# Attention's softmax work in larger pieces with two visits each, the last values projections moved to the end, and ScalarE's order fixed

## The chip, the cores and the metric

The program runs on one core of a Trainium2 chip. The metric is the device time of one execution in microseconds. Of three runs of the kernel before, the median is 2897.22 us (2896.98 to 2899.64). The core's engines are TensorE (PE in the profile, its weight loads PEld), VectorE (DVE), ScalarE (ACT), GpSimd (POOL) and SyncE (SP), which issues the DMAs here. Each engine works through its own list of instructions in the order in which they stand, and waits for others by semaphores.

## The reference

Two decoder layers over a sequence of 1024 tokens of width 1024, all in float32. Layer 0 mixes tokens by dilated sliding-window attention, layer 1 by a gated linear recurrence; behind each mixer stands a squared-ReLU MLP, and behind each of the four sub-layers `x <- LayerNorm(alpha * x + sublayer(x))`. The change lies in the attention:

```python
proj = (x @ w_in).reshape(B, S, 3, 3, 16, 64)        # 3 groups x (q, k, v) x 16 heads x 64
for g, (window, dilation) in enumerate(((128, 1), (512, 4), (2048, 16))):
    q, k, v = rotary(proj[:, :, g, 0]), rotary(proj[:, :, g, 1]), proj[:, :, g, 2]
    # sequence regrouped by residue mod dilation, in blocks of 128 queries;
    # a block sees itself and the block before it in its class
    s = where(in_band, q_block @ k_two_blocks.T / 8, -inf)
    m = max(s); p = exp(s - m); l = sum(p); o_g = (p / l) @ v_two_blocks; lse_g = m + log(l)
o = sum_g softmax_g(lse) * o_g                       # mixed per position and head
y = o @ w_out
```

## The kernel before

**Layout.** Heads are taken in 8 pairs of 128 rows (`NPAIR`). A *unit* is one pair in one of the three groups, so there are 24 units (`units`, L321), in the order group 2 (dilation 16), 1, 0 of pair 0, then of pair 1, and so on. Every unit has eight blocks of 128 queries. In group 2 a block sees only itself (128 keys); in group 1 every second block, and in group 0 all but the first, see 256 keys (`has_prev`, L464).

**Projections.** Two units make a group of work (L322). It needs six projections, taken as three pairs (keys and queries of the first unit, of the second, and the values of both), and each pair is computed with seven block products instead of eight (`ORDA`, L330). So `seq` (L331) has 12 groups x 7 x 3 = 252 products; the loop L732 takes one in a *slot*. A product is 12 matmuls of 128x512 (L646 to L648: each factor is split into a high and a low part of float32r, and three of the four partial products are kept). The x operands (`xh`, `xl`) of each of the seven are computed once, stored to DRAM (`xtd`) and loaded again for every later group (`get_T`, L375), 2 MB for each. Weights are loaded eight slots ahead, and split five slots ahead into a high part by ScalarE (L419) and three slots ahead into a low part by VectorE (L427).

**Inner work.** `pieces` (L461) cuts a unit into six pieces, which `at` hangs onto slots (`OFFS`, L55) of the next group: scores of two blocks (`qk`, L477, tile `s`), on VectorE mask, negative maximum and score in one instruction (L496), on ScalarE the exponential with its sum (L499), then the transposition of the probabilities on TensorE (`ptr`, L503, tile `ppt`) and its copy by ScalarE (L512), then the product with the values (`pv`, L515, tile `o`), copied to `og` by ScalarE (L532, L535). Values are transposed as well (`vtrans`, tile `vpt`). Maximum and sum are transposed (`combine_tr`, tile `mpt`), sent through DRAM to a layout with heads on rows, and `combine` (L566) makes of them the weights of the three groups, which six DMAs put into `frow`. `combine_mul` (L600) spreads them over the rows with a matmul (tile `fb`) and multiplies and adds on VectorE. PSUM has eight banks: three for the products (`mm`), two `s`, two `pt`, one `o`.

**The end.** The last group's two units can't begin before its projections are done. Their rotary steps, scores and all that follows (`tail`, L684, and the list `mine`, L782) are handed to `outproj_ln` (L849), which calls one entry at a time between the matmuls of the output projection (L179 to L181).

**What sets the order.** Inside the attention `in_order` (L103, L718) fixes TensorE and VectorE to the order in which the program writes the instructions; ScalarE, the DMAs and everything after the attention are placed by a scheduler.

## Time and profile before

| what | value |
|---|---|
| median of three runs | 2897.22 us |
| the profiled execution, its own time | 2893.09 us |
| span of its trace, first to last instruction | 2891.2 us |
| TensorE busy; its weight loads | 2785.1 us (96%); 2243.6 us (78%) |
| VectorE, ScalarE, GpSimd busy | 2084.2, 1450.7, 462.1 us |
| mean granted TensorE clock | 0.987 |
| attention's products (L646 to L648) | 7.98 to 1002.5 us |
| inner work, up to the last `fb` | 102.2 to 1097.5 us |

A timeline row has the start, the duration, the engine, the source line, the operation, what it writes and reads, and a count of instructions that were merged. In brackets stands the engine's idle time ahead of it and what ended that. Matmuls overlap, so the spacing of starts tells more than durations: a 128x512 matmul behind another starts 0.227 us after it at the full clock and 0.427 us after it at half. A float32 matmul of the inner work leaves two records in the trace; a transposition leaves one.

### The profile page before, as it was taken

The page shows a single profiled execution, that of the slowest core. Times are in us where ns is not written, and L with a number is a line of the kernel's source. Part 1 is how long each engine was busy: PE and PEld are TensorE (multiplying, and loading weights), DVE is VectorE, ACT ScalarE, POOL GpSimd, SP SyncE. Part 2 cuts the span into 40 slices and gives each one's busy share as a digit, 9 for nine tenths or more (in the row PEclk, how much of TensorE's full clock was granted, in tenths as well). Part 3 has the DMA queues.
Part 4 walks back from the last instruction along what each step waited for, and adds up shares of the span by engine and source line. Part 5 has one row for each costly group of instructions (what it writes and reads, how often), then busy time and mean ns, then how long its engine had stood idle before and what let it go on. Part 6 is the DMA issues. An engine that isn't in the chain of part 4 may idle for free. (4 is left out here: it accounts for less than half of the span.)

```text
span 2891.2 us, 40330 instructions
## 1 busy us (share of the span) xinstructions
PE 2785.1 (96%) x14152; PEld 2243.6 (78%) x14152; DVE 2084.2 (72%) x3685; ACT 1450.7 (50%) x3104; POOL 462.1 (16%) x211
## 2 busy tenths in 40 slices
PE   7899999999999998999999999999999999999998
PEld 6677777777777766788877887788888788877887
DVE  7677676777777667786688777456567787678777
ACT  5354555555455553645454434455553644454433
POOL 0111111111111102100053511111001200025310
PEclk9999999999999998999999999999999999999999
DMA  8876776678577533364484653111131455484654
GB/s 334 304 262 195 245 250 240 227 272 284 184 243 260 196 101 127 136 219 160 157 313 131 229 174 108 44 59 55 52 121 67 159 200 175 157 272 160 225 177 136
DMA packets 218043, 535.63 MB, mean 185 GB/s; under 512 B 30832, under 2 KB 45168, under 8 KB 217840
## 3 DMA queue, kind: packets, MB, share of 16 engines
q1 hardware_dynamic: 217840, 533.05, 54.1%
q8 instruction: 111, 1.82, 0.3%
q14 instruction: 92, 0.75, 0.1%
HBM read 408.96 MB, written 98.44 MB: 175 GB/s over the span
## 5 line engine op out<-in xcount | busy, mean ns | idle before, releaser
L646 PE MATMUL pmm<-xh,H 128*128 128x512 f32 x1008 | 410.2, 407 | 13.6 <-ACT H L419 8.0
L647 PE MATMUL pmm<-xl,H 128*128 128x512 f32 x1008 | 399.5, 396 | 12.3 <-DMA xl<-xtd 11.8
L648 PE MATMUL pmm<-xh,H 128*128 128x512 f32 x1008 | 398.6, 395 | 1.2 <-DVE H L427 1.2
L457 POOL TENSOR_TENSOR rot<-rot,sinT 128x1024 f32<-128x1024 f32 x48 | 137.7, 2873 | 861.0 <-DMA rot<-e 485.4
L646 PEld LDWEIGHTS pmm<-xh,H 128*128 128x128 f32 x1008 | 192.8, 191 | 54.6 <-ACT H L419 8.0
L647 PEld LDWEIGHTS pmm<-xl,H 128*128 128x128 f32 x1008 | 192.7, 191 | 52.6 <-DMA xl<-xtd 14.4
L648 PEld LDWEIGHTS pmm<-xh,H 128*128 128x128 f32 x1008 | 191.9, 190 | 43.8 <-DVE H L427 2.2
L496 DVE CUSTOM_DVE_ANT_0 p<-s,mask 128x128 f32<-128x128 f32 (+1 forms) x384 | 113.2, 348 | 142.3 <-PE s L485 132.5
L1226 PE MATMUL pdy<-dT,dS 128*128 128x512 f32 x512 | 201.4, 393 | 11.2 <-DVE dT L134 11.1
L499 ACT ACTIVATE p<-p,stats 128x128 f32<-128x128 f32 (+1 forms) x384 | 169.1, 443 | 65.9 <-DVE stats L496 65.5
L1227 PE MATMUL pdy<-dT,dS 128*128 128x512 f32 x512 | 200.6, 392 | 0.0
L1223 PE MATMUL pdy<-dT,dS 128*128 128x512 f32 x512 | 200.5, 392 | 0.0
L133 ACT ACTIVATE dS<-dr 128x512 fp32r<-128x512 f32 x192 | 120.1, 625 | 101.7 <-PE pdy L1227 45.3
L134 DVE TENSOR_TENSOR dS<-dr,dS 128x512 fp32r<-128x512 f32 x192 | 156.6, 815 | 10.7 <-ACT dS L133 10.7
L512 ACT ACTIVATE pts<-ppt 128x256 f32<-128x256 f32 (+1 forms) x192 | 85.9, 474 | 144.8 <-PE ppt L509 142.0
L167 PE MATMUL pmm<-f0nh,wh 128*128 128x512 f32 x384 | 152.7, 398 | 0.0
L169 PE MATMUL pmm<-f0nh,wl 128*128 128x512 f32 x384 | 150.4, 392 | 0.0
L168 PE MATMUL pmm<-f0nl,wh 128*128 128x512 f32 x384 | 149.8, 390 | 0.0
L1208 POOL TENSOR_TENSOR hold<-hold 128x512 f32<-128x512 f32 x32 | 52.2, 1632 | 568.3 <-DVE dT L134 290.8
L134 DVE TENSOR_TENSOR dT<-hold,dT 128x512 fp32r<-128x512 f32 x128 | 123.8, 967 | 3.7 <-ACT dT L133 3.7
L1226 PEld LDWEIGHTS pdy<-dT,dS 128*128 128x128 f32 x512 | 97.1, 190 | 32.9 <-DVE dT L134 12.9
L133 ACT ACTIVATE dT<-hold 128x512 fp32r<-128x512 f32 x128 | 80.2, 626 | 82.5 <-POOL hold L1202 33.5
(395 smaller groups left out, 7178.6 us busy)
## 6 DMA issues: line engine op xcount, KB each, us to landing
xh<-xtd SPq DMA_DIRECT2D x154, 512.0 KB
xl<-xtd SPq DMA_DIRECT2D x154, 512.0 KB
dr<-hd SPq DMA_DIRECT2D x192, 256.0 KB
dr<-in_w_down_dram SPq DMA_DIRECT2D x128, 256.0 KB
rot<-e SPq DMA_DIRECT2D x192, 128.0 KB
wa<-in_w_up_dram SPq DMA_DIRECT2D x48, 512.0 KB
wa<-in_w_attn_dram SPq DMA_DIRECT2D x36, 512.0 KB
wb<-in_w_attn_dram SPq DMA_DIRECT2D x36, 512.0 KB
```

Of the source, the lines that this page charges most:

```text
L133: act(hi, raw, AF.Copy)
L134: nc.vector.tensor_sub(lo, raw, hi.bitcast(F32))
L167: nc.tensor.matmul(o, wh[:, k], xs.h(k), start=k == 0, stop=False)
L168: nc.tensor.matmul(o, wh[:, k], xs.l(k), start=False, stop=False)
L169: nc.tensor.matmul(o, wl[:, k], xs.h(k), start=False, stop=k == NK - 1)
L499: act(p[:, h, :n], p[:, h, :n], AF.Exp, bias=sS[:, 0, h, b:b + 1], scale=-1.0, accum_out=sS[:, 1, h, b:b + 1])
L646: nc.tensor.matmul(o, wh, hi[k // 2][:, c], start=begin and k == 0, stop=False, skip_group_check=True)
L647: nc.tensor.matmul(o, wh, lo[k // 2][:, c], start=False, stop=False, skip_group_check=True)
L648: nc.tensor.matmul(o, wl, hi[k // 2][:, c], start=False, stop=end and k == 3, skip_group_check=True)
L1223: nc.tensor.matmul(o[q], h, T_[:, L], start=begin, stop=False, skip_group_check=True)
L1226: nc.tensor.matmul(o[q], h, T_[:, R], start=False, stop=False, skip_group_check=True)
L1227: nc.tensor.matmul(o[q], l, T_[:, L], start=False, stop=end, skip_group_check=True)
```

## The change

1. `Inner` takes the place of `pieces`. A unit of group 2 is one piece of eight blocks, the others are two pieces of four. Each piece has two visits: `visit_a` (the product with the values of the piece before, then all scores of this piece, in two `s` and two `pt` banks; VectorE and ScalarE take its first half in this slot and its second half in the next), and `visit_b`, two to four slots later (all transpositions of the piece, with two blocks of 128 keys in one bank; ahead of the first piece's products the values' transpositions; behind the last piece the transposition of maximum and sum). 
2. The groups of products: the first ten hold three pairs as before, the next two only the keys and queries of two units each, and a thirteenth the values of the last four units. 252 products are left, but the x operands are loaded for 13 groups. The last four units keep their transposed probabilities in `ptk` tiles and run only the values' part behind the attention.
3. ScalarE's order is fixed as well, with the exception of the high parts of the weights (`loose`), which are emitted one slot later than before.
4. `combine` has five steps instead of three, and its last tile comes from the large pool; `fb` uses the `s` banks and `mpt` the `o` bank. The `p` and `pts` pools have four buffers instead of three, the large pool 49 instead of 50.

```diff
-NSLOT = 50
+NSLOT = 49
-MIX = (5, 6, 7, 10, 11, 12, 13, 14, 15)
+MIX0, NMIX = 3, 5
-OFFS = ((0, 2, 4, 7, 9, 11), (10, 12, 15, 17, 19, 21))
+LATER = {9: 1, 10: 1, 11: 3}
-    wp = ctx.enter_context(tc.tile_pool(name="wp", bufs=3))
+    wp = ctx.enter_context(tc.tile_pool(name="wp", bufs=4))
...
-        groups = [units[i:i + 2] for i in range(0, len(units), 2)]
+        groups = [[("qk", u), ("qk", u + 1), ("v", u)] for u in range(0, len(units) - 4, 2)]
+        groups += [[("qk", u), ("qk", u + 1)] for u in (len(units) - 4, len(units) - 2)]
+        groups.append([("v", len(units) - 4), ("v", len(units) - 2)])
...
+            def banks(self, c):
+                bl = self.chunks[c]
+                if self.g == 2:
+                    return [bl[k:k + 2] for k in range(0, 8, 2)]
+                if self.g == 1:
+                    return [(bl[0], bl[2]), (bl[1],), (bl[3],)]
+                return [(b,) for b in bl]
...
+            def qk(self, c):
+                qT, kT = res[self.u, 0], res[self.u, 1]
+                for half, bl in enumerate(self.halves(c)):
+                    sb = [bank("pt" if half else "s", "s") for _ in range(2)]
...
+            def pv(self, c):
...
+                for b in self.chunks[c]:
+                    if b % 4 == 0:
+                        o = bank("pt" if g == 2 and b else "o", "o")
...
-            act(fh, l, AF.Copy)
-            yield
+            f2 = U("f", F32R)
+            fh = f2[:16, :NG * P].rearrange("p (g t) -> p g t", t=P)
+            fl = f2[:16, 512:512 + NG * P].rearrange("p (g t) -> p g t", t=P)
+            yield
+            act(fh, l, AF.Copy)
+            yield
...
-                fb = bank("pt", "fb")
+                fb = bank("s", "fb")
...
+        def visit_a(u, c):
+            while pend:
+                pend.pop(0)()
+            inner[u].qk(c)
+            inner[u].soft(c, 0)
+
+        def visit_b(u, c):
+            w = inner[u]
+            w.ptr(c)
+            if not w.hold:
+                if c == 0:
+                    w.vtrans()
+                pend.append(lambda: w.pv(c))
+            if c == len(w.chunks) - 1:
+                w.stats()
...
+            base, length = begin_of[gi + 1], begin_of[gi + 2] - begin_of[gi + 1]
+            hold = us[0] >= len(units) - 4
+            todo = [(u, c) for u in us for c in range(1 if units[u][1] == 2 else 2)]
+            for k, (u, c) in enumerate(todo):
+                first = base + UNIT0 + LATER.get(gi, 0)
+                a = first + k * length // len(todo)
+                b = first + int((k + 0.57) * length / len(todo) + 0.5)
+                if c == 0:
+                    at(a, lambda u=u, hold=hold: begin_unit(u, hold))
+                at(a, lambda u=u, c=c: visit_a(u, c))
+                at(a + 1, lambda u=u, c=c: inner[u].soft(c, 1))
+                at(b, lambda u=u, c=c: visit_b(u, c))
...
-        order = in_order((mybir.EngineType.PE, mybir.EngineType.DVE))
+        order = in_order((mybir.EngineType.PE, mybir.EngineType.DVE, mybir.EngineType.Activation), loose)
```

**TensorE, the second unit (group 1 of the first pair).** Names: `s` scores, `ppt` transposed probabilities, `vpt` transposed values, `o` product with the values, `mpt` transposed maximum and sum; "..." stands for the products (`pmm`) between the visits. Before, its first ten inner rows:

```order
L485 MATMUL s<-kT,qT 128x128 x2
L485 MATMUL s<-kT,qT 128x256 x2
L473 MATMUL vpt<-ident,vT 128x128 x8
...
L524 MATMUL o<-pts,vn 64x128 x4
...
L485 MATMUL s<-kT,qT 128x128 x2
L485 MATMUL s<-kT,qT 128x256 x2
L509 MATMUL ppt<-ident,p 128x128 x6
...
L550 MATMUL mpt<-ident,stats 32x128
...
L524 MATMUL o<-pts,vn 64x128 x6
L485 MATMUL s<-kT,qT 128x128 x2
```

Now, the same unit's first piece and the beginning of its second:

```order
L572 MATMUL o<-pts,vn 64x128 x16
L507 MATMUL s<-kT,qT 128x128 x2
L507 MATMUL s<-kT,qT 128x256 x2
L507 MATMUL s<-kT,qT 128x128 x2
L507 MATMUL s<-kT,qT 128x256 x2
...
L538 MATMUL ppt<-ident,p 128x128 x12
L556 MATMUL vpt<-ident,vT 128x128 x8
...
L572 MATMUL o<-pts,vn 64x128 x12
```

The runs have become two to four times as long and stand in fewer places between the products; a visit begins either with `o` or `s`, or with transpositions alone.

**ScalarE, the first group of products.** `H` is the high part of the weights, `xh` that of x, `e` a product copied out of PSUM, `bsel` a constant copied once, `hc_e` one of the other layer's constants. Before:

```order
L419 ACTIVATE H<-wb 128x512
L440 ACTIVATE bsel<-selw 128x384
L673 ACTIVATE e<-pmm 128x512
L419 ACTIVATE H<-wb 128x512
L133 ACTIVATE xh<-xT_296 128x1024
L673 ACTIVATE e<-pmm 128x512
L133 ACTIVATE xh<-xT_297 128x1024
L1384 ACTIVATE hc_e<-hc_e 128x16
```

Now:

```order
L430 ACTIVATE H<-wb 128x512
L133 ACTIVATE xh<-xT_294 128x1024
L133 ACTIVATE xh<-xT_295 128x1024
L720 ACTIVATE e<-pmm 128x512
L430 ACTIVATE H<-wb 128x512
L720 ACTIVATE e<-pmm 128x512
L720 ACTIVATE vp<-pmm 128x512
L430 ACTIVATE H<-wb 128x512 x2
...
L452 ACTIVATE bsel<-selw 128x384
```

The copy of `bsel` has moved back behind the products of two more of the seven steps, and both `xh` stand ahead of the copies out of PSUM.

**TensorE, behind the attention's last product.** The products left out ("...") are those of the output projection. Before, around the last transposition of maximum and sum and the last weights' matmuls:

```order
L509 MATMUL ppt<-ident,p 128x128 x4
L524 MATMUL o<-pts,vn 64x128 x8
L550 MATMUL mpt<-ident,stats 32x128
L524 MATMUL o<-pts,vn 64x128 x8
...
L606 MATMUL fb<-frow,bsel 128x512 x3
...
L606 MATMUL fb<-frow,bsel 128x512 x2
```

Now, from the last transposition of maximum and sum:

```order
L591 MATMUL mpt<-ident,stats 32x128
L538 MATMUL ppt<-ident,p 128x128 x4
L572 MATMUL o<-ptk,vn 64x128
L538 MATMUL ppt<-ident,p 128x128 x4
L572 MATMUL o<-ptk,vn 64x128 x15
L650 MATMUL fb<-frow,bsel 128x512 x2
...
L572 MATMUL o<-ptk,vn 64x128 x12
...
L572 MATMUL o<-ptk,vn 64x128 x14
...
L572 MATMUL o<-ptk,vn 64x128 x16
...
L650 MATMUL fb<-frow,bsel 128x512 x2
```

Between `mpt` and the `fb` that need its result there stood 42 matmuls of the output projection and 8 of `o`; now 72 of the output projection stand there, 70 of `o`, 16 transpositions and five `fb` of the pair before.

## Rows read from the trace of the kernel before

**Rows 1.** The page's first part: busy time by engine.
```profile
PE 2785.1 (96%) x14152; PEld 2243.6 (78%) x14152; DVE 2084.2 (72%) x3685; ACT 1450.7 (50%) x3104; POOL 462.1 (16%) x211
```

**Rows 2.** TensorE's waits, 105 to 1002 us: total, times, longest.
```profile
PE o L524 <- ACT og L535: 9.8, 3, 3.8
PE pmm L647 <- DMA xl<-xtd: 4.9, 4, 2.0
PE ppt L509 <- ACT pts L512: 4.5, 6, 1.4
PE vpt L473 <- DVE og L607: 3.6, 3, 1.6
```

**Rows 3.** Timeline of TensorE: one visit with three kinds of work.
```profile
127.42 0.39 PE L648 MATMUL pmm<-xh,H 128*128 128x512 f32 x1
127.74 0.66 PE L524 MATMUL o<-pts,vn 128*64 128x128 f32 x8
128.33 0.71 PE L485 MATMUL s<-kT,qT 64*128 64x128 f32 x8
128.98 0.66 PE L509 MATMUL ppt<-ident,p 128*128 128x128 f32 x4
129.39 0.48 PE L646 MATMUL pmm<-xh,H 128*128 128x512 f32 x1
129.71 0.40 PE L647 MATMUL pmm<-xl,H 128*128 128x512 f32 x1
```

**Rows 4.** Timeline of TensorE: a longer run of `o`.
```profile
225.77 1.09 PE L524 MATMUL o<-pts,vn 128*64 128x128 f32 x16
226.79 0.50 PE L646 MATMUL pmm<-xh,H 128*128 128x512 f32 x1
```

**Rows 5.** Timeline of TensorE: one transposition alone between products.
```profile
151.32 0.39 PE L648 MATMUL pmm<-xh,H 128*128 128x512 f32 x1
151.55 0.27 PE L550 MATMUL mpt<-ident,stats 128*32 128x128 f32 x1
...
151.89 0.40 PE L647 MATMUL pmm<-xl,H 128*128 128x512 f32 x1
```

**Rows 6.** Timeline of ScalarE and TensorE, 254 to 258 us.
```profile
254.22 0.52 ACT L591 ACTIVATE fh<-ml 16x384 fp32r<-16x384 f32 x1 [4.29 <-DVE ml L587]
...
256.71 1.04 ACT L535 ACTIVATE og<-o 128x512 f32<-128x512 f32 x1
...
257.80 1.12 PE L524 MATMUL o<-pts,vn 128*64 128x128 f32 x8 [3.79 <-ACT og L535]
```

**Rows 7.** Timeline of ScalarE and TensorE, 39 to 46 us.
```profile
39.23 0.52 ACT L440 ACTIVATE bsel<-selw 128x384 fp32r<-128x384 f32 x1 [6.88 <-DMA selw<-in_bsel_dram]
...
41.75 0.80 PE L646 MATMUL pmm<-xh,H 128*128 128x512 f32 x1 [2.36 <-ACT xh L133]
43.01 0.79 PE L647 MATMUL pmm<-xl,H 128*128 128x512 f32 x1 [0.47 <-DVE xl L134]
...
45.05 0.79 PE L648 MATMUL pmm<-xh,H 128*128 128x512 f32 x1 [1.24 <-DVE H L427]
```

**Rows 8.** Busy time by stretch: PE, PEld, DVE, ACT, POOL, clock, DMA share, GB/s.
```profile
0.00:100.00 100.00, 77.49 (x300) 60.88 (x300) 75.56 (x107) 39.55 (x61) 10.02 (x13) 0.93 0.91 337
300.00:400.00 100.00, 100.00 (x597) 78.29 (x596) 69.58 (x149) 57.65 (x157) 10.96 (x4) 1.00 0.74 256
1080.00:1100.00 20.00, 12.72 (x30) 7.05 (x29) 14.75 (x30) 5.03 (x9) 0.00 (x0) 0.65 0.41 130
```

**Rows 9.** Timeline of TensorE: the last maximum and sum, and the first weights.
```profile
1072.74 0.28 PE L550 MATMUL mpt<-ident,stats 128*32 128x128 f32 x1
...
1092.38 1.19 PE L606 MATMUL fb<-frow,bsel 128*128 128x512 f32 x2 [2.12 <-DMA frow<-fl]
```

**Rows 10.** VectorE and ScalarE by line and shape, 105 to 1002 us.
```profile
L496 DVE CUSTOM_DVE_ANT_0 p<-s,mask 128x256 f32<-128x256 f32 x154 | 57.6, 423 | 36.3 <-PE s L485 36.1
L535 ACT ACTIVATE og<-o 128x512 f32<-128x512 f32 x28 | 30.3, 1081 | 40.9 <-PE o L524 40.9
```

More of the change, by code (lines that the diff above doesn't have):

```diff
@@ L114, in __exit__ @@
             for i in list(nc.cur_bb.bb.instructions)[self.first:]:
-                if i.engine in self.engines:
+                if i.engine in self.engines and i.name not in self.loose:
                     if i.engine in before:
@@ L469, in vtrans @@
                 for j in range(2):
-                    pt = bank("pt", "vpt")
+                    pt = bank("s", "vpt")
                     for i in range(4):
@@ L503, in ptr @@
-            def ptr(b):
-                p = st.pop(("p", b))
-                nb = 2 if has_prev(b) else 1
-                pt = bank("pt", "ppt")
-                for h in range(2):
-                    for i in range(nb):
-                        nc.tensor.transpose(pt[:, (h * nb + i) * P:(h * nb + i + 1) * P],
-                                            p[:, h, i * P:(i + 1) * P], ident)
-                pts = wp.tile([P, 512], F32, name="pts", tag="pts")
-                act(pts[:, :2 * nb * P], pt[:, :2 * nb * P], AF.Copy)
-                st["pt", b] = pts
@@ L547, in combine_tr, with stats @@
+            def stats(self):
+                combine_tr(self.pr, self.g, self.sS, ml[self.pr])
         def combine_tr(pr, g, sS, ml):
-            pt = bank("pt", "mpt")
+            pt = bank("o", "mpt")
             nc.tensor.transpose(pt[:32, 0:P], sS.rearrange("p w a b -> p (w a b)"), ident)
@@ L564, in combine_tr, with combine @@
                             md[w, h].rearrange("(r i n) -> i r n", r=d, i=8))
-        def combine(pr, ml):
+        def combine(pr, ml, frow):
             def cv(tl, g):
@@ L621, in attention, with at @@
         fill = {}
-        def at(slot, f):
-            fill.setdefault(slot, []).append(f)
+        def at(slot, f, first=False):
+            fill.setdefault(slot, []).insert(0 if first else len(fill.get(slot, [])), f)
         ep, acc, part = {}, {}, {}
@@ L691, in unit_work @@
                 ogs[pr] = [None] * NG
-            sS = small([P, 2, 2, 8], "stats", 3)
-            adds = {}
-            def rope_of(t):
-                res[a, t], adds[t] = rope(ep.pop((gi, a, 0 if t == 1 else 1)), g, "qT" if t == 0 else "kT")
-            def begin():
-                ogs[pr][g] = U("og")
-                p = pieces(pr, g, res.pop((a, 0)), res.pop((a, 1)), ep.pop((gi, 2, a)), ogs[pr][g], sS)
-                for f in p[0]:
-                    f()
-                work.extend(p[1:])
@@ L706, in unit_work @@
-            work = []
-            later = [lambda: [f() for f in work.pop(0)] for _ in range(5)]
-            stats = [lambda: combine_tr(pr, g, sS, ml[pr])]
-            mix = []
-            if g == GORD[-1]:
-                steps = combine(pr, ml[pr])
-                mix = [lambda: next(steps, None)] * 3
-                for hb in range(2):
-                    muls = combine_mul(pr, ogs[pr], hb)
-                    mix += [lambda muls=muls: next(muls, None)] * 3
-            return adds, rope_of, [begin] + later, stats, mix
@@ L718, in attention, with begin_mix @@
-        order = in_order((mybir.EngineType.PE, mybir.EngineType.DVE))
+            inner[u] = Inner(u, hold)
+        def begin_mix(pr):
+            if pr == NPAIR - 1:
+                frows[pr] = U("frow", F32R)
+                nc.gpsimd.memset(frows[pr].bitcast(F32), 0.0)
+            steps = combine(pr, ml[pr], frows.get(pr, frow))
+            muls[pr] = [lambda: next(steps, None)] * NMIX
+            for hb in range(2):
+                m_ = combine_mul(pr, ogs[pr], hb, frows.get(pr, frow))
+                muls[pr] += [lambda m_=m_: next(m_, None)] * 3
@@ new lines, in attention @@
+        last_stats, visits = {}, set()
+        for gi, items in enumerate(groups):
+            us = [u for kind, u in items if kind == "qk"]
+            if not us:
+                continue
+            base, length = begin_of[gi + 1], begin_of[gi + 2] - begin_of[gi + 1]
[10 more added lines that the diff above has]
+                at(b, lambda u=u, c=c: visit_b(u, c))
+                last_stats[u] = b
+                visits |= {a, b}
@@ new lines, in attention @@
+        for pr in range(NPAIR):
+            t = last_stats[3 * pr + 2]
+            at(t + 2, lambda pr=pr: begin_mix(pr))
+            slots = [t + MIX0 + k for k in range(NMIX)]
+            if pr < NPAIR - 2:
+                slots += [n for n in range(slots[-1] + 2, slots[-1] + 20) if n not in visits][:6]
+            for k, n in enumerate(slots):
+                at(n, lambda pr=pr, k=k: muls[pr][k](), True)
+        order = in_order((mybir.EngineType.PE, mybir.EngineType.DVE, mybir.EngineType.Activation), loose)
@@ L785, in attention @@
+        mine += [[lambda k=k: muls[p7][k]()] for k in range(NMIX, NMIX + 6)]
         lists = [done[k:k + 1] + (mine[k] if k < len(mine) else []) for k in range(max(len(done), len(mine)))]
```

261 lines of the change are left out of this document (142 added, 119 removed).

## Prediction

> **What bounds the kernel now.** I read the page's busy times first, then TensorE's waits, then its timeline between two products. TensorE is busy 96% of the span and the next engine 72% [rows 1], so the time is TensorE's list plus its waits. In the attention's middle the waits sum to 23 us of 897 [rows 2], which by itself would leave a change of order little to win. But busy is not the same as useful: the timeline shows what an interruption of the products costs with no idle time in it. From the last product to `o` 0.32 us pass (127.42 to 127.74) where the next product would follow after 0.227, so 0.09 are lost; from the first product behind the visit to the second 0.32 pass again, 0.09 lost [rows 3]. A run of `o` with 8 records takes 0.59 us (127.74 to 128.33) [rows 3], one with 16 takes 1.02 (225.77 to 226.79) [rows 4]: 0.054 for a record and 0.16 for having a run. Transpositions take 0.10 each (0.41 for 4) and nothing for the run [rows 3]. A transposition alone between products moves the second product behind it by 151.89 - 151.32 - 2 x 0.227 = 0.116 us, so entering and leaving with a transposition costs only 0.02 [rows 5]. The end of the attention is the other place: from 1080 to 1100 us TensorE is busy 12.7 of 20 us at a clock of 0.65 [rows 8], and its wait ends with a DMA of `frow` [rows 9].
>
> **Fewer and longer runs.** Counted in TensorE's order up to the first layer norm, the number of inner matmuls and transpositions stays the same, and so do the 3024 product matmuls. What falls is the number of visits that begin with `o` or `s`, from 132 to 44; those with transpositions alone rise from 9 to 41; runs of `o` fall from 99 to 42 and runs of `s` from 96 to 40. Visits: 132 x 0.18 + 9 x 0.02 = 23.9 us before, 44 x 0.18 + 41 x 0.02 = 8.7 now, -15. Runs of `o`: 57 x 0.16 = -9. For a run of `s` no row splits the 0.65 us (128.33 to 128.98) into a fixed part and one for each of its four pairs: if a pair cost only what a pair of `o` records costs (0.107), 0.22 would be fixed, if nothing is fixed, zero. 56 runs make 0 to -12. The runs of `o` and `s` of 8 records are alike (0.59 and 0.65), which speaks for a fixed part in `s` as well, but part of the 0.65 may belong to the change to transpositions behind it; I take the middle, -6. Sum -30. Bounds: -19 if a visit that opens with transpositions costs 0.18 like the others (32 x 0.16 = 5 less) and `s` nothing, -36 with all of `s`.
>
> The Trainium skill, "TensorEngine Tiling (Array Packing)", section Key Properties, says that changing the tiling mode drains the array. By that rule a run of `s` (64 rows) behind `o` (64 columns) would pay like a run of `o` does, 56 x 0.16 = 9 instead of 6, and the sum would be 3 us lower. The trace agrees where it can be split (transpositions on the full array cost nothing extra); for `s` no row here decides.
>
> **Waits that go.** Three times TensorE waits for a copy of `og` (9.8 us) [rows 2]. The row shows why: ScalarE sits 4.29 us in `combine`'s copy `fh`, waiting for VectorE, with the exponentials and the `og` copy behind it [rows 6]. Now that copy has a slot of its own behind VectorE's work, and `og` copies of a piece stand directly behind its matmuls. The matmuls behind it run at half clock (8 records of `o` take 1.12 us there [rows 6], 0.66 else [rows 3]), an estimate of 1 us for each of the three: -13. The six waits for `pts` (4.5 us) come from two `pt` banks shared by successive transpositions; a visit now has four banks: -4. The waits of `vpt` for `fb`'s reader (3.6): -2, as `fb` moves to the `s` banks and finds readers there as well. Sum -19, between 0 (new waits of the same kind in their place) and -25.
>
> **Start.** ScalarE waits 6.88 us for the DMA of `selw` with the `xh` split behind it, and TensorE then waits 2.36 + 0.47 + 1.24 = 4.1 us and runs at half clock in between (43.01 to 45.05 and on) [rows 7]. In the changed order `bsel` stands behind two more steps of products: -6 (0 to -7). What is late next is the load of the x operands, which is as before.
>
> **End.** The last unit's maximum and sum take 19.6 us from `mpt` to the first `fb` that needs them (1072.74 to 1092.38) [rows 9], over DRAM twice. There 42 product matmuls cover 9.5 us of it. Now 72 products (16.3 us), 70 matmuls of `o` (7.5), 16 transpositions (1.6) and five `fb` (1.1) stand in between, 26.5 us: covered, with 7 to spare. The loss there was 7.3 us idle and some 5 us of half clock (35% of the 12.7 busy [rows 8]). I take -10 (0 to -12), the rest being lost to the late half of the last piece's scores, whose transpositions now follow with only one run of `o` and one of `vpt` ahead of them.
>
> **What the change adds.** (a) In group 2 the second half of `o` takes a `pt` bank, and the next piece's second half of scores needs it. A run of 16 matmuls of `o` takes 1.7 us by the rates above, a copy 1.08 [rows 10]; two copies back to back end some 3.2 us after the run began, the scores want the bank after 2.6: 7 x 0.6 = +4 (0 to 8). (b) Transpositions of a piece come 2 to 4 slots behind its scores. VectorE needs for a piece of group 0 eight times at most 0.51 us (0.423 and 0.084 for the accumulator's read, partly beside the next) [rows 10], 4 us; three products are 8.2 us, and VectorE is busy 70% with everything [rows 8], of which the softmax is a part. It fits on average and not always: 40 such visits at 0.2 us, +8; no row of before has such a wait, so the bounds are 0 and 40 (1 us each, as long as the average wait for `pts` and half of that for `xl` [rows 2]). Behind a waiting transposition stand the next products. (c) Three groups of 14 slots instead of two of 21 load the x operands once more, and faster: 2.1 MB for two slots instead of three. With weights and rotary copies that is about 2.7 MB in 8.5 us, 315 GB/s, against 256 in the middle of before and 337 reached in the first 100 us [rows 8]. It fits barely: 21 sets at 0.3 us, +6, between 0 and 25 (as long as the longest wait of before, 2.0 us, in half of them [rows 2]). (d) In the last short group transpositions come two slots behind the scores: four pieces at 1 us, +3 (0 to 6). Sum +21 (0 to 79). VectorE's, ScalarE's and GpSimd's own work is the same, apart from some 50 copies of `pts` fewer, which are off the path.
>
> **Sum.** -30 - 19 - 6 - 10 + 21 = -44 us. The profiled execution took 2893.1 us, of which 1.9 lie outside the span; that makes 2849, and as the median of the runs is 4.1 us above the profiled execution, 2853 us.
>
> **Rivals.** (1) Slower: the transpositions wait for the softmax in every visit. VectorE is fixed in order; scores now come in bursts of 2.8 to 4 us, and rotary steps, weights' low parts and sums stand ahead of them. For it: VectorE's 70%; against it: it idled for scores 36 us on the one shape alone [rows 10], so it is ahead of TensorE, not behind. The other terms without (b) give -52; from 40 visits x 1.45 us = 58 on the kernel is slower. At 1.8 us each: 2897 - 52 + 72 = 2917 us. (2) The three short groups are bound by DMA: if no more than the 256 GB/s of the middle flows, a set of 2.7 MB takes 10.5 us instead of 8.5, 21 x 2 = 42 instead of 6: 2889 us, about the edge of what can be told from no change. For it: waits for `xl` exist with three slots of lead already [rows 2]; against it: 337 GB/s in the first stretch. (3) The change does not do what it says on TensorE: the fixed costs move into the longer runs (a piece of `o` and `s` alternates between halves of the array as before), the -30 shrink to -5: 2878 us. For it: no run of this length is in the trace; against it: 8 and 16 records of `o` lie on one line with 0.16 at zero.
>
> **Chances.** The forecast, 2830 to 2872: 0.62. (1) 0.10, (2) 0.08, (3) 0.18, others 0.02. A measurement can tell about 0.2% from no change, 5.8 us. Forecast and (3) are faster, and half of (2): faster 0.83, same 0.06, slower 0.11. The range that holds 8 in 10 takes the forecast with the bound of all gains and (3): 2824 to 2888.
>
> **What would show it.** In the changed profile the spacing between products around a visit stays 0.32 and 0.32 while there are 85 visits; `s`, `o`, `ppt` keep their sums. TensorE's waits have no `o <- og` of 3 us in the middle and no `frow` at the end; 39 to 46 us has no `xh` wait; the attention's last product ends some 25 us earlier although the last values come last. A list of waits with `ppt <- ACT p` or `pmm <- DVE H` of over 40 us would make (1) right; `pmm <- DMA xl` over 30 us behind the tenth group (2); equal TensorE time without new waits (3). The prediction is wrong if the time is above 2888.

## The result and the profile after

The changed kernel took 2907.5 us (median of 6 runs) against 2898.4 for the kernel before in the same series: a ratio of 1.0029, 95% interval 1.0016 to 1.0042. It is slower by 8 to 9 us. 2853 was predicted, with 2888 as the upper end of the range. The profiled execution took 2906.5 us (2893.1 before, which is 5 us below the median of that kernel's runs: the two profiles lie 13 us apart where the medians lie 9).

The page's first part, the row that answers to [rows 1]:

```profile
PE 2766.2 (95%) x14152; PEld 2264.4 (78%) x14152; DVE 2086.8 (72%) x3685; ACT 1440.5 (50%) x3056; POOL 453.7 (16%) x212
```

TensorE's instructions are as many and it is busy 19 us less, as the change intends; yet the span is 13.5 us longer. So it stands still 32 us more. The view of busy time by stretch shows where. Its columns are as in [rows 8]; the stretches are the start, the middle, the time up to the attention's last product, and from there to the first layer norm. First the kernel before:

```profile
0.00:110.00 110.00, 85.27 (x337) 67.49 (x338) 85.49 (x125) 44.56 (x75) 12.41 (x14) 0.92 0.92 338
110.00:860.00 750.00, 728.40 (x4287) 569.28 (x4286) 539.70 (x1138) 406.09 (x1114) 104.81 (x36) 0.99 0.72 243
860.00:1002.10 142.10, 139.60 (x818) 109.14 (x817) 99.86 (x226) 81.69 (x224) 16.16 (x7) 1.00 0.68 230
1002.10:1121.00 118.90, 106.63 (x564) 76.74 (x563) 85.02 (x194) 53.16 (x143) 12.79 (x5) 0.91 0.29 90
```

And the changed one, in which the three short groups run from about 860 to 1050 us:

```profile
0.00:110.00 110.00, 87.42 (x366) 70.00 (x367) 87.72 (x133) 45.23 (x81) 11.28 (x14) 0.92 0.94 341
110.00:860.00 750.00, 708.01 (x4189) 579.10 (x4187) 527.20 (x1115) 395.47 (x1058) 102.32 (x35) 0.97 0.72 239
860.00:1050.40 190.40, 158.16 (x874) 125.28 (x875) 134.94 (x301) 95.97 (x278) 30.13 (x9) 0.93 0.79 268
1050.40:1141.50 91.10, 89.75 (x573) 71.76 (x572) 62.10 (x131) 40.97 (x92) 5.75 (x3) 1.00 0.32 111
```

A stretch loses in two ways: idle time (length less busy) and work at half the clock (1.2 GHz instead of 2.4). The second I take from the trace's clock records, to a tenth of a microsecond, as half of TensorE's busy time under a granted clock of 0.50; the two-digit clock of the rows agrees with it.

| stretch | before: idle, half clock | after: idle, half clock | change |
|---|---|---|---|
| start, to 110 us | 24.7, 6.6 | 22.6, 7.1 | -1.6 |
| middle, 110 to 860 | 21.6, 6.0 | 42.0, 17.9 | +32.3 |
| to the last product (1002.1; 1050.4) | 2.5, 0.0 | 32.2, 10.1 | +39.8 |
| to the first layer norm (1121.0; 1141.5) | 12.3, 8.2 | 1.4, 0.0 | -19.1 |
| sum | 61.1, 20.8 | 98.2, 35.1 | +51.4 |

What remains, work at full clock, is 1121.0 - 61.1 - 20.8 = 1039.1 us before and 1141.5 - 98.2 - 35.1 = 1008.2 now: -30.9. In the twelve kernels of the experiments, all made from the changed one, the same figure lies between 1008 and 1014 us, so this saving is 25 to 31 us whatever the waits are. The first layer norm comes 20.5 us later = 51.4 - 30.9. Behind it the changed kernel wins some 7 us back in code that the change doesn't touch.

How far one execution can lie from another shows e2 below: up to 860 us TensorE and VectorE work through the same lists there as in the changed kernel, and its middle has 43.5 us idle and 11.1 at half clock instead of 42.0 and 17.9. A difference of a few us of idle time, or of 7 us of half clock, is no finding by itself.

TensorE's waits in the changed kernel from 105 to 1050 us, which answer to [rows 2] (the engine, what waited for what; total us, times, longest):

```profile
PE pmm L691 <- DMA xl<-xtd: 22.3, 11, 6.1
PE vpt L556 <- ACT pts L545: 11.7, 10, 3.5
PE pmm L690 <- ACT H L430: 8.3, 2, 5.0
PE fb L650 <- DMA frow<-f: 7.9, 3, 3.3
PE s L507 <- DVE kT L471: 7.7, 3, 3.1
PE ppt L538 <- DVE og L651: 6.9, 4, 3.3
PE pmm L692 <- DVE H L439: 4.4, 5, 2.1
PE s L507 <- ACT og L582: 1.4, 3, 0.6
```

The `o <- og` of [rows 2] are gone. In their place are waits around the mixing of heads (`vpt`, `fb`, `s`, `ppt`: 36 us) and for loads and weights (`xl` and `H`: 35 us). The first kind, in the timeline of the changed kernel (start, length, engine, line, idle time before and what ended it):

```profile
365.39 0.54 DVE L623 TENSOR_TENSOR ml<-ml 16x384 f32<-16x384 f32 x1
...
367.75 0.85 DVE L629 TENSOR_TENSOR ml<-ml,mn 16x128 f32<-16x128 f32 x3
...
368.69 0.52 ACT L635 ACTIVATE f<-ml 16x384 fp32r<-16x384 f32 x1 [3.06 <-DVE ml L629]
369.12 1.05 ACT L545 ACTIVATE pts<-ppt 128x512 f32<-128x512 f32 x2
...
369.75 0.33 PE L556 MATMUL vpt<-ident,vT 128*128 128x128 f32 x1 [3.52 <-ACT pts L545]
```

ScalarE stands 3.06 us in front of `combine`'s copy `f`, until VectorE has ended its step of `combine`; that step alone takes 3.2 us (365.39 to 368.60), more than the 2.7 us of a slot's twelve products. The copies `pts` are ready but stand behind it in ScalarE's fixed list; `vpt` needs the bank that they empty. This is the stall of [rows 6], with `pts` in the place of `og`. The second kind, a wait of SP, its list behind that wait, and TensorE, all in the third short group:

```profile
SPq L603 <- DVE f L637: 6.5, 1, 6.5
...
1010.65 1.39 SPq L603 DMA_DIRECT2D ml<-mdram  x4
...
1012.47 4.00 SPq L641 DMA_DIRECT2D frow<-f  x6
...
1020.92 1.64 SPq L393 DMA_DIRECT2D xl<-xtd  x2
...
1027.91 0.79 PE L691 MATMUL pmm<-xl,H 128*128 128x512 f32 x1 [6.06 <-DMA xl<-xtd]
1028.51 0.63 PE L692 MATMUL pmm<-xh,H 128*128 128x512 f32 x1
1028.93 0.63 PE L690 MATMUL pmm<-xh,H 128*128 128x512 f32 x1
```

The load is issued late. SP first stands 6.5 us in front of `ml`, until VectorE is through with `f`; then it issues `ml` and `frow` (4.0 us for six), and in the place of the third dots two loads of `xh` and six for the output projection. TensorE goes on 7.0 us after `xl` was issued. The products behind the wait then follow each other in 0.42 us instead of 0.227: the granted clock is 0.50 there, the level of 1.2 GHz. Between 110 and 1050 us the clock records have 15 such falls, each beside a wait of 2.0 to 6.1 us; three other waits of 2.1 to 3.3 us (at 256, 931 and 1016 us) have none. Before there were 3 falls up to 1002 us. That is why the half-clock column grew with the idle one.

### The profile page after: what moved, and what is told of

Read it like the earlier page. It is cut to its first block, busy times and chain, and to the rows that moved or that the text cites. A ratio compares the mean times of both kernels' runs of the same rounds, so it can differ in the third digit from the quotient of the medians.

```text
span 2904.7 us, 40321 instructions
## 1 busy us (share of the span) xinstructions
PE 2766.2 (95%) x14152; PEld 2264.4 (78%) x14152; DVE 2086.8 (72%) x3685; ACT 1440.5 (50%) x3056; POOL 453.7 (16%) x212
## 3 DMA queue, kind: packets, MB, share of 16 engines
HBM read 423.64 MB, written 98.44 MB: 180 GB/s over the span
## 5 line engine op out<-in xcount | busy, mean ns | idle before, releaser
L691 PE MATMUL pmm<-xl,H 128*128 128x512 f32 x1008 | 405.8, 403 | 32.4 <-DMA xl<-xtd 32.4
L690 PE MATMUL pmm<-xh,H 128*128 128x512 f32 x1008 | 412.3, 409 | 22.6 <-ACT H L430 16.3
L692 PE MATMUL pmm<-xh,H 128*128 128x512 f32 x1008 | 404.7, 402 | 4.5 <-DVE H L439 4.4
L690 PEld LDWEIGHTS pmm<-xh,H 128*128 128x128 f32 x1008 | 196.4, 195 | 75.0 <-ACT H L430 19.1
L692 PEld LDWEIGHTS pmm<-xh,H 128*128 128x128 f32 x1008 | 196.0, 194 | 50.2 <-DVE H L439 8.2
L1116 ACT ACTIVATE H<-wc 128x512 fp32r<-128x512 f32 x128 | 77.3, 626 | 74.3 <-DVE wc L1109 43.7
```

Source lines behind the costliest of these rows:

```text
L690: nc.tensor.matmul(o, wh, hi[k // 2][:, c], start=begin and k == 0, stop=False, skip_group_check=True)
L691: nc.tensor.matmul(o, wh, lo[k // 2][:, c], start=False, stop=False, skip_group_check=True)
L692: nc.tensor.matmul(o, wl, hi[k // 2][:, c], start=False, stop=end and k == 3, skip_group_check=True)
```

## The experiments

The median, and the ratio to runs of the kernel before on the same chip, with its 95% interval. The changed kernel stands at 1.0029. As series ran on several chips, kernels are compared below by their ratios; 0.1% is 2.9 us. Idle time and half clock are always those of the profiled execution.

| run | median us | ratio | interval |
|---|---|---|---|
| e1, ScalarE not pinned | 2945.0 | 1.0167 | 1.0153 to 1.0180 |
| e2, groups of three | 2902.5 | 1.0025 | 1.0014 to 1.0036 |
| e3, three small DMAs on GpSimd | 2903.9 | 1.0027 | 1.0015 to 1.0038 |
| e4, mixing spread | 2889.5 | 0.9977 | 0.9966 to 0.9987 |
| e5, e4 and four small DMAs on GpSimd | 2895.2 | 1.0000 | 0.9989 to 1.0010 |
| e6, e4 and last groups of three | 2877.6 | 0.9940 | 0.9928 to 0.9952 |
| e7, e4 and visits one slot later | 2906.1 | 1.0034 | 1.0022 to 1.0046 |
| e8, e6 and rotary multiply on VectorE | 2872.1 | 0.9923 | 0.9909 to 0.9936 |
| e9, e6 and two small DMAs on GpSimd | 2881.3 | 0.9954 | 0.9940 to 0.9968 |
| e10, e8 and e9 together | 2876.9 | 0.9940 | 0.9926 to 0.9954 |
| e11, e8 and keys' rotary work earlier | 2871.1 | 0.9924 | 0.9910 to 0.9939 |
| e12, copy `f` alone not pinned | 2900.9 | 1.0014 | 1.0005 to 1.0022 |

### e1: the pin on ScalarE

```
-order = in_order((PE, DVE, Activation), loose)
+order = in_order((PE, DVE))
```

> The changed kernel with ScalarE's order left to the scheduler again; VectorE and TensorE stay fixed. Theory A (the pin puts combine's copy f, which waits 3 to 4 us for VectorE, ahead of the copies pts, and vpt on TensorE waits for those): the waits vpt<-pts (11.7 us, 10 times, the longest 3.5) fall below 4 us, half-clock time behind them goes too, and the kernel takes 10 to 20 us less than the changed one (2907), about 2890 to 2897. Rival B (the pin is not what costs: without it the scheduler places the same copies no better, and the softmax's exponentials may come later): within 5 us of 2907, or slower if H copies or exponentials move behind waiting instructions.

`vpt<-pts` fell to 2.6 us as theory A said, and the kernel became 1.4% slower, 40 us. Other work now came late. Of TensorE's waits from 105 to 1080 us this one grew most, from 1.4 us (`pmm<-DVE H` from 4.4 to 13.8):

```profile
PE s L507 <- ACT og L582: 19.0, 6, 5.4
```

Theory A was right on the wait and wrong on the time: the pin as a whole is worth 40 us to these larger pieces. What it may still cost in one place, e12 asks.

### e12: only the copy `f` out of the pin

```
 act(fh, l, AF.Copy)
+loose.add(nc.cur_bb.bb.instructions[-1].name)
```

> The changed kernel (2907.5) with combine's copy f alone left out of ScalarE's fixed order; at every second mixing it then stands behind the copies pts instead of ahead of them, at the others it stays. Theory A (the place that the pin gives f is what vpt waits for): the two or three waits vpt<-pts of 3.5 us go, vpt<-pts falls from 11.7 to about 4 us, and with the half clock the time falls by 5 to 10 us: 2897 to 2902. Rival B (VectorE's dense steps are the cause, and a later copy f makes the rows of frow late instead): fb<-frow grows from 7.9 to over 12 us, and the time is within 4 us of 2907.5.

`vpt<-pts` fell to 4.4 us over the attention, none over 1.2, as theory A said, and `fb<-frow` was 7.3 instead of 7.9. But TensorE's idle time did not follow. The middle, and up to the first layer norm 96.1 us in all instead of 98.2:

```profile
110.00:860.00 750.00, 708.02 (x4249) 579.27 (x4249) 537.78 (x1132) 398.67 (x1065) 109.78 (x36) 0.99 0.72 243
```

That is 42.0 us idle, as in the changed kernel; over the attention `xl` waits 26.4 us instead of 22.3 and `pmm<-DVE H` 6.5 instead of 4.4. Half clock in the middle fell from 17.9 to 9.4, little more than two executions of one order can differ. The time is 0.15% less (4 us, 6.6 by the medians) and in theory A's range, with intervals that overlap. So the place of `f` is shown to be what `vpt` waited for; that it costs time is not shown.

### e4: combine's steps two slots apart

```
-slots = [t + MIX0 + k for k in range(NMIX)]
+slots = [t + MIX0 + k * (2 if pr < NPAIR - 2 else 1) for k in range(NMIX)]
```

> The changed kernel with the five steps of combine two slots apart instead of one (for the first six pairs of heads; fb's steps move back by four slots or more). Theory A (the steps are too dense for VectorE, whose chain of 3 to 4 us a step holds ScalarE's copy f and then pts, and SP's frow issues): vpt<-pts falls from 11.7 to below 3 us, fb<-frow from 7.9 to below 1, and with the half clock behind these waits (about as much again) the kernel gains 15 to 25 us: 2882 to 2892. Rival B (VectorE's list is too full around mixing whatever the spacing, and the same work only delays other instructions): the waits move to s<-kT, ppt<-og or pmm<-DVE H with the same sum, and the time stays within 5 us of 2907.

0.52% less than the changed kernel, 15 us, and faster than the kernel before. In the middle idle time fell from 42.0 to 34.3 and half clock from 17.9 to 6.2. TensorE's largest waits there, 105 to 860 us:

```profile
PE s L507 <- DVE kT L471: 10.7, 7, 2.4
PE pmm L692 <- DVE H L439: 9.3, 6, 3.6
PE vpt L556 <- ACT pts L545: 6.2, 8, 1.5
```

`fb<-frow`, `ppt<-og` and the two waits for `xl` of 3 to 4 us are gone, `vpt<-pts` is halved. Theory A holds; rival B has a share, as `kT` and `H` took back 11 of the 26 us (a wait of 5 us for ScalarE's `H`, at 842 us here, lies behind 860 in the changed kernel and is left out of this). The two `xl` waits belonged to the mixing too: in the changed kernel SP stood 9.4 and 8.2 us in front of the store `ond<-og`, which waits for the last multiply, with the load behind it.

### e7: visits one slot later

```
-UNIT0 = 3
+UNIT0 = 4
```

> The kernel with combine's steps two slots apart and every visit one slot later in its group. In the spread kernel the scores wait 14.8 us (8 times) for the rotary sum kT, which VectorE gets to late while it mixes; the first piece's scores stand one slot behind that sum. Theory A (the distance is what is missing): s<-kT falls below 4 us and the kernel gains 8 to 14 us with the half clock: 2876 to 2882. Rival B (VectorE is behind by more than a slot and whatever follows it waits instead): s<-kT stays above 8 or pmm<-DVE H takes its place, within 4 us of 2889.5.

`s<-kT` fell from 14.8 to 6.2 us, but `s<-og` rose to 16.3 (three of 4.8 to 4.9 us, at every second mixing) and `pmm<-H` from 9.3 to 21.6: 0.57% slower than e4, 17 us, which neither theory had. Rival B in kind: other waits took the place, and the visit met another step of the mixing.

### e2: groups of three

```
-groups = [[("qk", u), ("qk", u + 1), ("v", u)] for u in range(0, len(units) - 4, 2)]
-groups += [[("qk", u), ("qk", u + 1)] for u in (len(units) - 4, len(units) - 2)]
-groups.append([("v", len(units) - 4), ("v", len(units) - 2)])
+groups = [[("qk", u), ("qk", u + 1), ("v", u)] for u in range(0, len(units), 2)]
...     # nothing is held, and the lists behind the last product follow
```

> The changed kernel with twelve groups of three pairs as before: no short groups, the last values projections are back beside the queries and keys, and the last two units' pieces run behind the last product. Theory A (three short groups cost by their own loads): the waits and half clock between 860 and 1050 us (32 idle and 10 of half clock) shrink to the level of the middle, some 10 and 4, which gives 28 us; the gain at the end (19 us against the kernel before) is lost again; the sum is 2907 - 28 + 19 = 2898. Rival B (the short groups are a general shortage of the attention's end, by SP's list or the last mixing steps, which a group of three would have as well): nothing comes back between 860 and 1050, the end is lost: 2920 to 2926.

Both halves of theory A came out, the second larger than expected (26 us, not 19). From 860 us to the last product, and from there to the first layer norm:

```profile
860.00:1013.00 153.00, 142.62 (x827) 116.22 (x825) 104.65 (x233) 78.29 (x212) 17.11 (x6) 0.97 0.60 206
1013.00:1137.50 124.50, 108.30 (x580) 82.32 (x579) 85.79 (x199) 56.72 (x151) 12.53 (x6) 0.90 0.30 95
```

Idle and half clock in the first are 10.4 and 5.1 instead of 32.2 and 10.1 (27 us back), in the second 16.2 and 11.5 instead of 1.4 and 0 (26 us lost). So the last values projections behind all queries and keys do cover the end, and the short groups that this took cost as much. In time the two cancel, 1.0025 against 1.0029.

### e3 and e5: small DMAs away from SP

```
-nc.sync.dma_start(...)      # mdram<-sr, ml<-mdram, frow<-f; in e5 also ond<-og
+nc.gpsimd.dma_start(...)
```

> The changed kernel with three kinds of small DMAs (mdram<-sr, ml<-mdram, frow<-f) issued by GpSimd instead of SP, so that no load of x operands or weights stands behind their waits. Theory A (loads come late because SP's list waits in front of them, 88 us in the middle and 27 in the short groups): the waits for xl, xh, and for H behind late weights (32 + 1 + 16 us over the attention) fall to about 15 us, fb<-frow (7.9) falls as well; 30 to 40 us less than 2907 with the half clock behind them: 2867 to 2877. Rival B (the short groups are limited by the bytes that DMA moves, 375 to 394 GB/s in some stretches): the waits for xl stay above 25 us and the time is 2897 to 2907.

> The kernel with combine's steps two slots apart, and all small DMAs (mdram<-sr, ml<-mdram, frow<-f, and also the store ond<-og, which alone held SP for 9.4 us before an xl load in the changed kernel) issued by GpSimd. Theory A (SP's list is what makes the short groups' loads late): the waits for xl (22.9 us, all but none of them in the short groups) and for H (7.2) fall to below 10 us together, and 860 to 1034 us lose some 20 of their 31 idle and 14 half-clock us: 2889.5 - 20 = about 2870. Rival B (bytes): in the short groups xl still sums to over 12 us, with loads that land later than they would have to although SP issued them at once; 2882 to 2892. Rival C (GpSimd's own list, where the rotary multiplies stand behind the new waits, takes over): s<-kT or s<-qT grow past 15 us, no gain.

In e3 `xl` fell from 22.3 to 14.6 us, two of 4 us behind `ond<-og` stayed, the short groups lost 30 us instead of 42; the middle lost 69 instead of 60, and the time is in rival B's range and not in theory A's. In e5 `xl` fell from 22.9 us in e4 to this:

```profile
PE pmm L691 <- DMA xl<-xtd: 1.3, 2, 1.2
```

The bytes read are the same 423.64 MB, and from 860 to 1034 us the DMA engines moved 49.8 MB in e5 and 43.3 in e4. So the bytes were not the limit of e4, the order of SP's list was. The Trainium skill, "DMA: Bandwidth & Descriptors", section "Anatomy of one DMA — SWDGE (gpsimd) path", has it that a DMA's wait for a semaphore is done by the issuing sequencer ahead of dispatch; the trace agrees. Yet e5 is 0.23% slower than e4. Its short groups lose 36 us instead of 45, not 20 less, and its middle 57 instead of 41; `fb<-frow` is 16.7 us in all, `pmm<-DVE H` 18.7 instead of 9.3. GpSimd's list is in order too, and in it (start, length, idle before):

```profile
899.50 1.90 POOL L641 DMA_DIRECT2D frow<-f  x3 [11.52 <-ACT f L635]
908.38 0.61 POOL L603 DMA_DIRECT2D ml<-mdram  x1 [6.99 <-DVE f L637]
...
915.61 1.24 POOL L641 DMA_DIRECT2D frow<-f  x2
916.87 2.35 POOL L469 TENSOR_TENSOR rot<-rot,sinT 128x1024 f32<-128x1024 f32 x1
919.16 0.60 POOL L641 DMA_DIRECT2D frow<-f  x1
```

The last rows of `frow` go out 20 us behind the first, behind `ml` and a multiply, and TensorE pays for it:

```profile
925.52 0.76 PE L650 MATMUL fb<-frow,bsel 128*128 128x512 f32 x1 [9.99 <-DMA frow<-f]
```

Rival C in kind (GpSimd's list takes over), though on `frow` and not on `kT`.

### e6: two last groups of three, with one unit behind

```
-groups += [[("qk", u), ("qk", u + 1)] for u in (len(units) - 4, len(units) - 2)]
-groups.append([("v", len(units) - 4), ("v", len(units) - 2)])
+groups += [[("qk", nu - 4), ("qk", nu - 3), ("qk", nu - 2)], [("qk", nu - 1), ("v", nu - 4), ("v", nu - 2)]]
...     # what is held, and the lists behind the last product follow
```

> The kernel with combine's steps two slots apart, in which the last three short groups become two groups of three: queries and keys of units 20 to 22, then those of 23 beside the last two values projections. x operands are loaded 12 times as in the kernel before. The last unit's two pieces run behind the last product, with the held pieces of 20 to 22 beside them. Theory A (the short groups' x loads cost 27 idle and 9 half-clock us there, and most of the end's gain comes from what covers the last unit's way over DRAM, which is still there): behind 860 us idle and half clock fall from 46.6 to some 25 us: 2889.5 - 22 = 2868. Rival B (with a unit behind the last product the end loses as much as with groups of three in the earlier run, 16 idle and 11 half clock): the time stays at 2885 to 2892.

Its two last stretches:

```profile
860.00:1003.20 143.20, 125.86 (x696) 101.06 (x695) 103.69 (x223) 74.01 (x209) 18.45 (x7) 0.93 0.63 208
1003.20:1107.60 104.40, 97.31 (x586) 75.83 (x585) 66.57 (x143) 44.54 (x105) 8.83 (x5) 0.97 0.32 107
```

Together 24.4 idle and 9.4 half clock, 34 us against 46.6 in e4; 0.37% less by the ratios, 11 us, half of theory A's 22. The profiled execution is 7 us below the median of its runs. With x operands loaded 12 times again and a cover for the last unit, the change wins 0.6% over the kernel before. Most of what remains is VectorE (`H`, `kT` and `stats`, 27 us; `xl` is 9.7):

```profile
904.55 2.35 POOL L469 TENSOR_TENSOR rot<-rot,sinT 128x1024 f32<-128x1024 f32 x1 [3.01 <-DMA rot<-e]
...
904.90 2.55 DVE L439 TENSOR_TENSOR H<-wa,H 128x512 fp32r<-128x512 f32 x1
...
907.50 0.79 PE L692 MATMUL pmm<-xh,H 128*128 128x512 f32 x1 [4.53 <-DVE H L439]
```

A subtraction that takes 0.68 us elsewhere lasts 2.55 beside GpSimd's multiply, and TensorE waits for it.

### e8, e9, e10, e11: VectorE, GpSimd and SP

```
-nc.gpsimd.tensor_mul(rot, rot, sinT)                     # in rope, e8
+nc.vector.tensor_mul(rot, rot, sinT)                     # ahead of the sum with rot
-nc.sync.dma_start(...)                                   # mdram<-sr and ond<-og, e9
+nc.gpsimd.dma_start(...)
-at(k + 2 + j, ... rope_of(u, 1)); at(k + 5 + j, ... add_of(u, 1))   # e11
+at(k + 1 + j, ... rope_of(u, 1)); at(k + 4 + j, ... add_of(u, 1))
```

> The kernel with spread mixing steps and last groups of three (2877.6), with the rotary multiply rot<-rot,sinT on VectorE, at the place of the sum that needs it, instead of on GpSimd. In the earlier profile VectorE's subtractions for H take 0.68 us alone and 1.50 on average (up to 2.8) where GpSimd's multiply of 2.4 us runs beside them, those that read a PSUM bank stay at 0.68. Theory A (GpSimd's multiply holds VectorE up for about its own length whenever VectorE works on SBUF alone, and this makes the backlog behind s<-kT, pmm<-DVE H and ppt<-stats, 27 us): 48 multiplies cost VectorE 1.2 us each now and give back about as much or more, s<-kT and pmm<-DVE H fall by half, the time falls by 5 to 15 us: 2863 to 2873. Rival B (VectorE gets 58 us more work in its list, in front of the scores that need kT): s<-kT grows by 1.2 us each, 2880 to 2895.

> The kernel with spread mixing steps and last groups of three (2877.6), with only the two DMAs that SP waits for longest (mdram<-sr, 174 us in the attention, and ond<-og, 45) issued by GpSimd; the loads of ml and the rows frow stay on SP. Theory A (SP's list is late, its waits cost; what spoiled the earlier run with all small DMAs on GpSimd was frow behind other work there): xl falls from 9.7 us to below 3, no wait of fb for frow comes up, and the time falls by 5 to 12 us: 2866 to 2873. Rival B (GpSimd's list with two long waits delays the rotary multiplies, and these VectorE's sums): s<-kT and pmm<-DVE H grow by as much as xl gives back, 2875 to 2885.

> Both of the former: the rotary multiply on VectorE, and mdram<-sr and ond<-og issued by GpSimd, which has nothing else to do then. If both theories A hold, the gains add, as nothing on GpSimd can be late: 2877.6 - 10 - 8 = about 2860. If only the DMAs' waits for GpSimd's multiplies are what spoils the second, this run is faster than the sum of the two apart. If VectorE is full, it is no faster than the second alone.

> The kernel with spread mixing steps, last groups of three and the rotary multiply on VectorE (2872.1), in which the rotary work of the keys starts and ends one slot earlier in each group, while the visits stay where they are. TensorE waits there 20.9 us (9 times) for kT at the first visit of a group, with VectorE busy without a gap before. Theory A (the sum only stands too close to the scores in VectorE's list): s<-kT falls below 4 us and the time by 12 to 20 us with the half clock behind these waits: 2852 to 2860. Rival B (VectorE is behind whatever the place: the low parts of H, which stand behind the rotary work now, come later instead): pmm<-DVE H grows from 9.8 to over 20 us, or VectorE waits for the DMA of rot, and the time stays above 2868.

e8: the time is in theory A's range, but its interval (up to 0.9936) overlaps that of e6 (from 0.9928), so the gain over e6 isn't settled. Where VectorE's busy time went is plain. Sums up to the first layer norm, of e6 and then of e8:

```profile
sum 1107.60, PE 1027.65 PEld 834.50 DVE 811.88 ACT 575.32 POOL 142.18; mean PE 256.91 PEld 208.62 DVE 202.97 ACT 143.83 POOL 35.54
```

```profile
sum 1103.50, PE 1026.06 PEld 831.92 DVE 807.97 ACT 575.52 POOL 8.18; mean PE 256.52 PEld 207.98 DVE 201.99 ACT 143.88 POOL 2.04
```

With GpSimd's 48 multiplies of 1.2 us added to its list VectorE is busy 4 us less, not 58 more. But `s<-kT` went as rival B said, from 9.2 to 20.9 us: the multiply now stands directly ahead of the sum. In the same run `xl` fell from 9.7 to 0.4 us, with SP's list as it was; which of SP's waits became shorter was not followed. e11 moved multiply and sum a slot up: `s<-kT` was gone, and `pmm<-H` went from 9.8 to 19.1 us, nearly its rival B (over 20). The time stayed: in the 8 us ahead of each of these waits of 0.8 us or more VectorE is 98 or 99% busy, so a place won for one instruction is lost by the next. e9 missed: `xl` fell to 2.1 us, `s<-kT` rose to 24.2 (in a profile 6 us above the median of its runs), and the time is rival B's. e10 is as fast as e6 and, within the intervals, as e9: with no multiply on GpSimd `s<-kT` is 15.8 and `xl` 5.6, more than the 0.4 of e8, whose DMAs stay on SP. e4, e6 and e8 to e11 beat both kernels; e8 and e11 are the fastest, 0.8% under the kernel before.

## Why the prediction was wrong

**Fewer and longer runs: right.** -30 was the term, -30.9 the change of work at full clock (it holds every kind of work, so a little of it may be something else). That the two lie within 1 us is chance, as the other kernels made from this one give 25 to 31. The spacing held:

```profile
154.42 0.39 PE L692 MATMUL pmm<-xh,H 128*128 128x512 f32 x1
154.74 1.53 PE L572 MATMUL o<-pts,vn 128*64 128x128 f32 x24
156.20 1.58 PE L507 MATMUL s<-kT,qT 64*128 64x128 f32 x16
157.71 0.50 PE L690 MATMUL pmm<-xh,H 128*128 128x512 f32 x1
158.04 0.39 PE L691 MATMUL pmm<-xl,H 128*128 128x512 f32 x1
...
230.32 2.06 PE L507 MATMUL s<-kT,qT 64*128 64x128 f32 x32
232.30 0.50 PE L690 MATMUL pmm<-xh,H 128*128 128x512 f32 x1
```

0.32 and 0.33 us around the visit, and 24 records of `o` in 1.46 us, where 0.16 + 24 x 0.054 gives 1.46. Rival 3 is out. What no row of before could split, the last two rows do: 32 records of `s` take 1.98 us, 8 of the same shape took 0.65 [rows 3] (the 16 at 156.20 hold wider ones as well), so a record takes 0.055 and a run of `s` about 0.2. It has a fixed part as `o` has. (Visits with transpositions alone were 17 before, not 9, which is worth 0.2 us.)

**Waits that go: the step that failed first.** -19 was the term; the middle alone lost 32 us more than before. The waits named did go (`o<-og`, `ppt<-pts`), but new ones came in their place, and more of them than the term's bound of 0 allowed for. The step said of `f`: "Now that copy has a slot of its own behind VectorE's work". A slot of its own in the program is 2.7 us behind the step before, and VectorE was not through with its 3.2 us; the wait stayed, and the pin put `pts` behind it. I followed which instruction stands ahead, and not when its operand is there. e4, which spreads the steps, gives 15 us back, 19 of the middle's 32 in idle time and half clock. e12, which moves this one copy, takes 7 us off `vpt<-pts` and next to nothing off the idle time. What the rest of the 32 us comes from was not separated.

**The three short groups (c): the term that was mis-sized most.** +6, at most 25; measured +40 (32.2 idle and 10.1 half clock against 2.5), which e2 confirms by taking the short groups out (27 us back). Of the 32.2 us idle the waits for `xl` are 15.1. Rival 2 had the place, and its size of 42 only by chance: it priced the bytes by a rate, and its own sign, `xl` over 30 us, did not come. e5 took the waits for `xl` away with the same bytes. The loads were issued late, since SP's list held waits for the statistics, the weights `f` and the store of the mixed heads ahead of them (e3, e5). I had counted what is moved, and not what stands in front of it. The other half of the idle time is waits for ScalarE's `H` (8.3; ScalarE in turn stands 2.8 and 2.9 us there for VectorE's sums of weights), for `og` (3.3), `kT` (3.1) and smaller ones; no experiment took these away alone.

**What the half clock costs.** The sum had it only in the waits that go, at the start and at the end. Of the 18 waits of 2 us or more between 110 and 1050 us, 15 have a stretch at 1.2 GHz beside them: +14 us beside +37 of idle time.

**End: right, and too small.** -10 expected, 0 to -12; -19.1 measured. The rows answering to [rows 9]:

```profile
1077.07 0.27 PE L591 MATMUL mpt<-ident,stats 128*32 128x128 f32 x1
...
1106.84 0.62 PE L650 MATMUL fb<-frow,bsel 128*128 128x512 f32 x2
```

The first weights that need the last maximum and sum are wanted 29.8 us behind it, and nothing waits. The step counted what was lost from 1080 to 1100 us, 12 us; the stretch from the last product to the first layer norm lost 20.5, and 8 of these lay outside that window. I had also left a rest for the late scores; nothing of it was there. e2, which undoes this part, loses 26 us there.

**Start: mostly wrong.** -6 expected, -1.6 measured. The 4.1 us of [rows 7] went; the waits for `xl` rose from 6.9 to 10.1 us, that for `e` from 3.3 to 4.5. "What is late next is the load of the x operands, which is as before", said the step: it was late next, and not as before.

**The other additions.** (a) `s<-og` is 1.4 us, +4 was taken. (b) `ppt<-p` is 0.2 us in all, +8 was taken: rival 1 is refuted, the transpositions hardly ever wait for the softmax. (d) No such wait came up.

**Behind the attention** the changed kernel is 7 us faster, in code that is the same; `pdy<-dT` fell from 11.1 to 6.5 us. All kernels made from it are 5 to 9 us faster there than the one profile of the kernel before. Why wasn't tried; no term had it.

The sum as it was: -31 + 32 + 40 - 19 - 2 - 7 = +13, the difference of the two profiled executions (9 by the medians). The attention's last product, forecast some 25 us earlier, ends 48 us later. The kernel is slower because what it added in waits (72 us) exceeds what it saved, although its two main savings, the fewer runs and the covered end, came out.

## What to carry to other kernels

When steps of one chain are put into consecutive slots of fixed lists, compare each step's duration on its engine with the slot's length before you count a wait as gone; in a pinned list the waiting instruction delays all that is behind it, and the wait only changes its name. Where loads share an in-order list with small DMAs that wait, price the waits that stand ahead of a load, and not only its bytes. And where VectorE is the engine behind most of the remaining waits, moving single instructions by a slot (e7, e11) only moved the wait here.

## What the runs showed of the hardware

GpSimd's multiply of 128 x 1024 (2.35 us and more) holds up VectorE where VectorE reads two operands from SBUF: in e6 the 36 subtractions for `H` that overlapped it took 1.57 us on average (0.66 to 2.90), the 216 others 0.68; additions with one operand in PSUM (`e<-pmm,e`) took 0.68 in both cases. The Trainium skill, "SBUF — State Buffer", section "SBUF: two separate sides", says that the two engines share a port pair, held by one for a whole instruction, which a VectorE operation with two SBUF inputs takes as well. The trace agrees: the subtraction shown under e6 ends 0.55 us behind the multiply that had begun first. e8 gives the price: with the multiplies moved to VectorE its busy time did not rise.

A DMA issued by GpSimd kept it 0.57 us on average (`frow`, `ml` in e5), and up to 5.7 us passed between two such issues with no wait that the profile shows (31.3 us in 11 cases).
